# Query and memory-value projections in halves of 256 columns, two token blocks to a PSUM bank

## The chip, the cores and the metric

The kernel runs on one core of a Trainium2 chip. The metric is the device time of one execution in microseconds (us); smaller is better. TensorE (PE in the profile) multiplies and writes PSUM, VectorE (DVE), ScalarE (ACT) and GpSimd (POOL) work on tiles, and SyncE (SP) issues most of the DMAs. PSUM has eight banks, each 128 partitions by 512 fp32 columns.

## The reference

Two layers of a trunk over 256 latent and 256 context tokens, model width 1024. Each layer is a half-step SwiGLU block, three token mixers in parallel on one normalised input, and another SwiGLU block. The mixers are a windowed attention (A), a dense attention with RMS-normalised queries and keys (B) and a chunked mLSTM (C); one combined projection feeds all of them:

```python
def windowed_attention(q, k, v, k_ctx, v_ctx, sink): ...
def dense_attention(q, k_all, v_all):
    return blockwise_queries(lambda args: gqa_softmax(args[0], k_all, v_all, None, None), q)
IN_SIZES = (A_WIDTH, A_KV_WIDTH, A_KV_WIDTH, B_WIDTH, B_KV_WIDTH, B_KV_WIDTH, C_WIDTH, C_WIDTH, C_WIDTH, C_WIDTH, 4 * C_HEADS, N_BRANCH * D_MODEL)
```

The change concerns two pieces of 512 columns of that projection: the queries of branch B (`qb`, 8 heads of 64), which are squared and summed per head for the norm and rotated, and the values of the mLSTM (`vm`, 4 heads of 128). All arithmetic is fp32: each operand is split into a high and a low part, and a product is three matmuls.

## The kernel before, in words

**Tasks and units.** The work is a list of tasks. A task names the weight units that it needs, and `run_tasks` walks the list: SyncE loads units ahead into four raw buffers (512 KB each, L152), ScalarE rounds one to its high part (L162), VectorE takes the low part (L163), and the task's function emits its matmuls. `mm3` (L191) emits the three matmuls of a product, at L193 to L195.

**Order.** The code emits tasks one after another, and a scheduler then sets the order of each engine's instructions at compile time; a tile's readers and writers wait for each other by semaphores. PSUM tiles are whole banks of a pool of eight (`self.psum()`).

**The two projections.** `tok_tasks` makes four tasks for `qb` and four for `vm`. Task g takes two of the eight 128-row blocks of the model width, at all 512 columns. For each token block tb (four in layer 0; in layer 1 the context queries are not needed, so `qb` has two) it adds 2 x 3 matmuls of 512 columns into that block's own bank. After the fourth task `evac` empties each bank: for `qb` `q_rows` copies it on ScalarE (L760), squares it on ScalarE (L761), sums the squares of a head on VectorE (L762), and rotates latent blocks (L741, L746 twice, L747) or scales context blocks by the norm's gain (L772). For `vm` one copy, by turns on ScalarE (L200) and VectorE (L202).

**The attention woven around them.** `attn_steps` makes steps for each branch, token block and pair of heads. Step i holds score i, the transposes of step i-2 (`ATT_LAG`) and the product with V of step i-3. A score is two or three matmuls per head (L1016, mask L1018, L1019), the row maximum on VectorE (L1020, L1023), the exponential on ScalarE (L1034), the sink's term and the sum (L1039 to L1041), its reciprocal on VectorE (L1043) and the scaling of both heads on GpSimd (L1046). TensorE then transposes the scaled rows (L1058), ScalarE and VectorE split them (L188, L189), and TensorE multiplies by V (L1073, L1075). The queries of branch A come to score step 0 through `q_cols` (L779 transposes, L784 ScalarE, L785 VectorE). In layer 0 the remaining `qb` tasks and all `vm` tasks are woven between the first steps, with the mLSTM's gates (L1110 to L1190) and the merge gates (transposed products `fm`, evacuated at L1327); in layer 1 `qb` comes earlier and `vm` stands there.

Of the kernel before, what the change touches and what calls it, by code (L numbers as in the profile page):

```python
# [62 lines left out]
class Builder:  # L63
# [41 lines left out]
    def unit_src(self, key):  # L105
# [16 lines left out]
        if kind == "tok":  # L122
            _, l, name, ks, n = key
            src = a["w_" + name][l, ks[0] * P:(ks[-1] + 1) * P, :]
            return src.rearrange("(k p) c -> p k c", p=P), (len(ks), n), True
        if kind == "fm":
            _, l, j = key
            return a["w_fm"][l, j], (NK, P), True
# [566 lines left out]
    def tok_tasks(self, l, name, n, kper, tbs, ms, evac):  # L695
# [24 lines left out]
        return [mk(g) for g in range(ngroups)]  # L720

    def by_stream(self, tasks, pre):

        def fn(units):
            later = []
            for u, (_, t) in zip(units, tasks):
                t([u], [0, 1], later)
            pre(1)
            for evac, tb, ps in later:
                evac(tb, ps)  # L730
            for u, (_, t) in zip(units, tasks):
                t([u], [2, 3])
        return [([k for ks, _ in tasks for k in ks], fn)]
# [15 lines left out]
    def q_rows(self, q, src, tb, branch, ss):  # L749


        nc = self.nc
        if branch == 0:
            if tb < 2:
                self.rope(q, src, 8, tb, self.cos, self.sin)
            else:
                self.copy(q, src)
            return
        sq = self.t512()
        nc.scalar.activation(out=q, in_=src, func=AF.Copy)  # L760
        nc.scalar.activation(out=sq, in_=src, func=AF.Square)  # L761
        nc.vector.tensor_reduce(out=ss, in_=sq.rearrange("p (h d) -> p h d", d=64), axis=AX.X, op=ALU.add)  # L762
        if tb < 2:
            u = self.t512()
            self.rope(u, q, 8, tb, self.cosg[0], self.sing[0], q)
        else:
            self.times_g(q, q, 8, 0)

# [61 lines left out]
    def mixer_tasks(self, l, need_ctx, ms, pre, done, turn):  # L830
# [20 lines left out]

        def qq(x):
            def f(tb, ps):
                if f"qr{x}" not in R:
                    R[f"qr{x}"] = self.slot([P, 4, T])
                    if x:
                        R["qss"] = self.lp.tile([P, 4, 8], F32, tag="qss", name=self.nm("qss"))
                self.q_rows(R[f"qr{x}"][:, tb, :], ps, tb, x, R["qss"][:, tb, :] if x else None)
            return f

# [23 lines left out]

        def vm(tb, ps):
            if "vm" not in R:
                R["vm"] = self.slot([P, 4, 4, 129])
                nc.vector.memset(R["vm"][:, :, :, 128:129], 1.0)
            self.copy(R["vm"][:, tb, :, 0:128], ps.rearrange("p (h d) -> p h d", h=4))

# [10 lines left out]
        vt = self.tok_tasks(l, "vvg", 272, 2, range(4), ms, vv)  # L901
        qa = self.tok_tasks(l, "qa", 512, 2, qtb, ms, qq(0))
        qb = self.tok_tasks(l, "qb", 512, 2, qtb, ms, qq(1))
        conv = [self.conv_task(l, c, ms, R, need_ctx) for c in range(8)]

# [3 lines left out]
        kk_ = self.tok_tasks(l, "kk", 256, 4, range(4), ms, kk)  # L909
        vm_ = self.tok_tasks(l, "vm", 512, 2, range(4), ms, vm)  # L910
        if need_ctx:
# [538 lines left out]
def _layout(inp):  # L1450
# [20 lines left out]
    a["w_qa"] = c(w[:, :, C_QA + qcols])  # L1471
    a["w_qb"] = c(w[:, :, C_QB + qcols])
    a["w_kk"] = c(np.concatenate([w[:, :, C_KA:C_KA + 128], w[:, :, C_KB:C_KB + 128]], axis=2))
    gcols = np.concatenate([np.arange(0, 4), np.arange(8, 12), np.arange(4, 8), np.arange(12, 16)])
    a["w_vvg"] = c(np.concatenate([w[:, :, C_VA:C_VA + 128], w[:, :, C_VB:C_VB + 128], w[:, :, C_GM + gcols]], axis=2))
    a["w_vm"] = c(w[:, :, C_VM:C_VM + 512])
    a["w_om"] = c(w[:, :, C_OM:C_OM + 512])
# [42 lines left out]
```

## Time and profile before

| | |
|---|---|
| time, median of 3 runs | 2246.11 us (2245.70 to 2246.91) |
| the profiled execution's own time | 2245.83 us |
| its span in the profile | 2244.0 us |
| TensorE busy | 2186.8 us, 97% |
| VectorE busy | 1546.0 us, 69% |
| ScalarE busy | 997.9 us, 44% |
| GpSimd busy | 135.4 us, 6% |
| mean granted clock of TensorE | 0.992 |

The span is what the profiler covers; the profiled execution took 1.8 us more than it. Busy shares are means over all stages. The granted clock is 1.00 at TensorE's upper level, 2.4 GHz, and 0.50 at the lower, 1.2 GHz. Times in rows are microseconds from the start of the span, unless a duration is marked as ns. The changed tasks of layer 0 run from about 472 us, those of layer 1 (`vm`) from about 1760 us.

### The profile page before, as it was taken

Reading aid. Unit: us, or ns where it says so; the run is one execution under the profiler, and the core shown is the slowest. Engines: PE = TensorE matmul, PEld = TensorE weight load, DVE = VectorE, ACT = ScalarE, POOL = GpSimd, SP = SyncE. Lnnn points to the kernel's source line nnn. Section 1 sums busy time; section 2 is a strip of 40 time slices with the busy share of each in tenths; the row PEclk is TensorE's granted clock in tenths of the full one; section 3 lists DMA queues with packets and bytes.
Section 4 is the critical chain, followed back from the end, with each engine's and each line's share of the span. In section 5 each row is a group of like instructions: output and inputs, shape, how many; then the busy total and the mean of one; then the engine's idle time right before and its main releaser. Section 6 shows DMA issues by size and latency. Waiting matters only on the chain.

```text
span 2244.0 us, 30646 instructions
## 1 busy us (share of the span) xinstructions
PE 2186.8 (97%) x11666; PEld 1833.2 (82%) x11666; DVE 1546.0 (69%) x2760; ACT 997.9 (44%) x1594; POOL 135.4 (6%) x100
## 2 busy tenths in 40 slices
PE   7999999999999999999999999999999999998998
PEld 4877777787888888888878788777778888997997
DVE  4987775778576775664444378878858887876556
ACT  3322223545577833542222253222236468855444
POOL 0000000013152000000000000000000152000000
PEclk9999999999999999999999999999999999998999
DMA  7765564321213334434434236555744214565664
GB/s 285 226 197 182 165 200 146 123 94 68 92 51 113 122 120 143 142 112 133 139 104 134 101 118 197 189 187 181 222 138 152 85 67 126 183 217 173 193 190 155
DMA packets 127555, 334.52 MB, mean 149 GB/s; under 512 B 12840, under 2 KB 26216, under 8 KB 126640
## 3 DMA queue, kind: packets, MB, share of 16 engines
q1 hardware_dynamic: 112240, 315.60, 43.4%
q10 hardware_dynamic: 15168, 16.97, 2.4%
q8 instruction: 91, 1.49, 0.3%
q14 instruction: 56, 0.46, 0.1%
HBM read 322.48 MB, written 10.04 MB: 148 GB/s over the span
## 4 chain that ended last, share of the span: by engine, by line
PE 89%; DVE 6%; ACT 2%; issue 1%; DMA 1%; ACTq 0%; DVEq 0%
PE ps L193 27%; PE ps L194 27%; PE ps L195 27%; PE ps L1259 1%; PE ps L1058 1%; PE ps L1228 1%; PE ps L366 1%; DVE lo L163 1%; PE ps L1073 1%; PE ps L468 1%; PE ps L1075 1%; PE ps L1016 1%; DVE sm L1020 1%; DMA slot<-in_w_ada_dram 1%; PE ps L1019 1%
## 5 line engine op out<-in xcount | busy, mean ns | idle before, releaser
L162 ACT ACTIVATE hi<-raw 128x1024 fp32r<-128x1024 f32 (+1 forms) x444 | 457.4, 1032 | 770.7 <-PE ps L194 255.9
L193 PE MATMUL ps<-slot,hi 128*128 128x512 f32 (+1 forms) x2232 | 778.4, 351 | 6.0 <-ACT slot L188 4.9
L194 PE MATMUL ps<-slot,hi 128*128 128x512 f32 (+1 forms) x2232 | 775.6, 348 | 0.7 <-DVE slot L189 0.5
L195 PE MATMUL ps<-slot,lo 128*128 128x512 f32 (+1 forms) x2232 | 773.6, 347 | 0.0
L163 DVE TENSOR_TENSOR lo<-raw,hi 128x1024 fp32r<-128x1024 f32 (+1 forms) x444 | 526.7, 1190 | 232.3 <-ACT hi L162 230.6
L193 PEld LDWEIGHTS ps<-slot,hi 128*128 128x128 f32 x2232 | 420.5, 189 | 75.9 <-ACT slot L188 6.2
L195 PEld LDWEIGHTS ps<-slot,lo 128*128 128x128 f32 x2232 | 421.5, 189 | 57.4
L194 PEld LDWEIGHTS ps<-slot,hi 128*128 128x128 f32 x2232 | 421.5, 189 | 56.3 <-DVE slot L189 2.0
L193 PE MATMUL ps<-hi,slot 128*128 128x512 f32 (+2 forms) x1048 | 400.3, 382 | 1.9 <-ACT slot L188 1.1
L195 PE MATMUL ps<-hi,slot 128*128 128x512 f32 (+2 forms) x1048 | 398.8, 381 | 0.0
L194 PE MATMUL ps<-lo,slot 128*128 128x512 f32 (+2 forms) x1048 | 398.8, 381 | 0.0
L358 DVE SCALAR_TENSOR_TENSOR t<-raw,sc,t 128x1024 f32<-128x1024 f32 x224 | 280.3, 1281 | 129.9 <-DMA raw<-in_w_ada_dram 129.7
L1046 POOL TENSOR_SCALAR t<-t,sm 128x512 f32<-128x512 f32 (+1 forms) x96 | 135.2, 1420 | 1748.1 <-DVE sm L1043 1693.2
L193 PEld LDWEIGHTS ps<-hi,slot 128*128 128x128 f32 x1048 | 197.1, 188 | 46.2 <-issue 6.6
L195 PEld LDWEIGHTS ps<-hi,slot 128*128 128x128 f32 x1048 | 196.7, 188 | 39.8
L194 PEld LDWEIGHTS ps<-lo,slot 128*128 128x128 f32 x1048 | 197.0, 188 | 38.9 <-issue 0.2
L188 ACT ACTIVATE slot<-t 128x512 fp32r<-128x512 f32 (+1 forms) x138 | 80.5, 594 | 172.3 <-DVE t L606 153.5
L606 DVE TENSOR_TENSOR t<-ps,t 128x512 f32<-128x512 f32 (+1 forms) x88 | 54.7, 622 | 86.5 <-PE ps L195 85.2
L189 DVE TENSOR_TENSOR slot<-t,slot 128x512 fp32r<-128x512 f32 (+1 forms) x138 | 87.6, 643 | 5.1 <-ACT slot L188 4.6
L1020 DVE TENSOR_REDUCE sm<-ps 128x1 f32<-128x512 f32 (+1 forms) x96 | 54.1, 593 | 29.6 <-PE ps L1019 29.0
L603 ACT ACTIVATE t<-ps 128x512 f32<-128x512 f32 (+1 forms) x88 | 46.4, 527 | 24.2 <-DVE t L426 16.5
L189 DVE TENSOR_TENSOR t<-ps,t 128x512 fp32r<-128x512 f32 x80 | 54.2, 684 | 1.9 <-ACT t L188 1.7
(195 smaller groups left out, 1667.7 us busy)
## 6 DMA issues: line engine op xcount, KB each, us to landing
raw<-in_w_gu_dram SPq DMA_DIRECT2D x176, 512.0 KB
raw<-in_w_ada_dram SPq DMA_DIRECT2D x128, 512.0 KB
raw<-in_w_down_dram SPq DMA_DIRECT2D x92, 512.0 KB
raw<-in_w_fm_dram SPq DMA_DIRECT2D x64, 512.0 KB
raw<-in_w_br_dram SPq DMA_DIRECT2D x24, 512.0 KB
raw<-in_w_out_dram SPq DMA_DIRECT2D x24, 512.0 KB
slot<-in_w_ada_dram SPq DMA_DIRECT2D x16, 512.0 KB
raw<-in_w_down_dram SPq DMA_DIRECT2D x20, 256.0 KB
```

The lines of the kernel that those rows point to most:

```text
L162: self.nc.scalar.activation(out=hi, in_=raw, func=AF.Copy)
L163: self.nc.vector.tensor_tensor(out=lo, in0=raw, in1=hi.bitcast(F32), op=ALU.subtract)
L188: self.nc.scalar.activation(out=hi, in_=src, func=AF.Copy)
L189: self.nc.vector.tensor_tensor(out=lo, in0=src, in1=hi.bitcast(F32), op=ALU.subtract)
L193: mm(out, lh, rh, start=start, stop=False, **kw)
L194: mm(out, lh, rl, start=False, stop=False, **kw)
L195: mm(out, ll, rh, start=False, stop=stop, **kw)
L358: v.scalar_tensor_tensor(out=acc, in0=units[0], scalar=c, in1=acc, op0=ALU.mult, op1=ALU.add)
L603: nc.scalar.activation(out=hs["sg"][:, :W], in_=ps[:, :W], func=AF.Silu)
L606: nc.vector.tensor_tensor(out=hid[:, :W], in0=ps[:, :W], in1=hid[:, :W], op=ALU.mult)
L1020: v.tensor_reduce(out=mx[:, e:e + 1], in_=ps[:, :nkey], axis=AX.X, op=ALU.max)
L1046: nc.gpsimd.tensor_scalar(out=t[:, :nkey], in0=t[:, :nkey], scalar1=r[:, e:e + 1], scalar2=None, op0=ALU.mult)
```

## The change

`qb` and `vm` are made by a new `half_tasks`. There are still four units of 512 KB each, but a unit now holds four 128-row blocks at 256 columns: unit (h, g) is column half h, rows g. For each half the two units follow each other, and the half is evacuated after the second. Token blocks 0 and 1 share a bank (256 columns each), and so do 2 and 3; only the first matmul into a bank carries the start flag. The evacuation works on 256 columns, 4 query heads or 2 value heads at a time. The weights are laid out so that a unit is one contiguous piece per partition.

```diff
+        if kind == "half":
+            _, l, name, h, g = key
+            return a["w_" + name][l, h, g], (4, 256), True
...
+    def half_tasks(self, l, name, tbs, ms, evac):
+        ds = {}
+        def mk(h, g):
+            def fn(units):
+                u = units[0]
+                for tb in tbs:
+                    if g == 0 and tb % 2 == 0:
+                        ds[h, tb // 2] = self.psum().rearrange("p (b c) -> p b c", b=2)
+                    ps = ds[h, tb // 2][:, tb % 2, :]
+                    for x in range(4):
+                        lh, ll = ms["hi"][g][:, x, tb * P:(tb + 1) * P], ms["lo"][g][:, x, tb * P:(tb + 1) * P]
+                        self.mm3(ps, lh, ll, u[0][:, x, :], u[1][:, x, :], g == x == tb % 2 == 0, g == 1 and x == 3,
+                                 skip_group_check=True)
+                    if g:
+                        evac(tb, h, ps)
+            return ([("half", l, name, h, g)], fn)
+        return [mk(h, g) for h in range(2) for g in range(2)]
...
-        sq = self.t512()
+        sq = self.t512()[:, :256]
...
-            self.rope(u, q, 8, tb, self.cosg[0], self.sing[0], q)
+            self.rope(u, q, 4, tb, self.cosg[0], self.sing[0], q)
...
-            self.times_g(q, q, 8, 0)
+            self.times_g(q, q, 4, 0)
...
-            self.copy(R["vm"][:, tb, :, 0:128], ps.rearrange("p (h d) -> p h d", h=4))
+            self.copy(R["vm"][:, tb, 2 * h:2 * h + 2, 0:128], ps.rearrange("p (h d) -> p h d", h=2))
...
-        qb = self.tok_tasks(l, "qb", 512, 2, qtb, ms, qq(1))
+        qb = self.half_tasks(l, "qb", qtb, ms, qqb)
...
-        vm_ = self.tok_tasks(l, "vm", 512, 2, range(4), ms, vm)
+        vm_ = self.half_tasks(l, "vm", range(4), ms, vm)
...
+    halves = lambda m: c(m.reshape(2, 2, 4, P, 2, 256).transpose(0, 4, 1, 3, 2, 5))
-    a["w_qb"] = c(w[:, :, C_QB + qcols])
+    a["w_qb"] = halves(w[:, :, C_QB + qcols])
-    a["w_vm"] = c(w[:, :, C_VM:C_VM + 512])
+    a["w_vm"] = halves(w[:, :, C_VM:C_VM + 512])
```

The scheduler then orders the engines differently. Line numbers of the changed kernel are 3 higher at `mm3` (L196 to L198), 25 higher in `q_rows` and `q_cols`, and 27 higher in the attention. The number of instructions on SyncE is the same; TensorE has 336 more matmuls in all, VectorE 26 more instructions, ScalarE 16 more.

*TensorE, layer 0, in front of the first transposes.* Before, from the first `qb` matmul on there are 72 matmuls of 512 columns and the three score steps 0 to 2, and these rows end that stretch; `ps_3834` is token block 3's bank of `qb`, `t_628` and `t_629` are the two heads' rows of step 0, which GpSimd has scaled:

```order
L195 MATMUL ps_3834<-hi_3920,slot_3117 128x512
L193 MATMUL ps_3834<-hi_3920,slot_3115 128x512
L194 MATMUL ps_3834<-lo_3921,slot_3115 128x512
L195 MATMUL ps_3834<-hi_3920,slot_3117 128x512
L1058 MATMUL ps_3976<-ident,t_628_3855 128x128 [waits PE_49,Activation_49,Pool_49]
L1058 MATMUL ps_3976<-ident,t_629_3857 128x128 [waits Pool_49]
L1058 MATMUL ps_3976<-ident,t_628_3855 128x128
L1058 MATMUL ps_3976<-ident,t_629_3857 128x128
L193 MATMUL ps_3813<-hi_4178,slot_3115 128x512
```

Now there are 72 matmuls of 256 columns and the same score steps. `ps_3838` is the bank of blocks 2 and 3, `ps_4029` and `ps_4034` are score step 2, and `t_626` and `t_627` are step 0's rows:

```order
L198 MATMUL ps_3838<-hi_3697,slot_3117 128x256
L1043 MATMUL ps_4029<-slot_3741,slot_3770 128x512 [waits DVE_49,PE_49]
L1045 MATMUL ps_4029<-maskr,identr 128x256
L1046 MATMUL ps_4029<-slot_3741,slot_3770 128x512
L1043 MATMUL ps_4034<-slot_3741,slot_3770 128x512 [waits DVE_49,PE_49]
L1045 MATMUL ps_4034<-maskr,identr 128x256
L1046 MATMUL ps_4034<-slot_3741,slot_3770 128x512
L1085 MATMUL ps_4054<-ident,t_626_3877 128x128 [waits PE_49,Pool_49]
```

The 16 `qb` matmuls that stood between score step 2 and the transposes have moved behind them; the transposes now follow score step 2 directly. Their waits (Pool, Activation) are the same.

*TensorE, layer 0, directly behind those transposes.* `ps_4075` is a merge gate of 512 columns and `ps_3813` the bank of token blocks 0 and 1, here block 1's second unit; before, no `qb` matmul of a first use waits in this way:

```order
L1085 MATMUL ps_4061<-ident,t_627_3879 128x128
L196 MATMUL ps_4075<-slot_3114,hi_3807 128x512 [waits PE_49,Activation_49]
L197 MATMUL ps_4075<-slot_3116,hi_3807 128x512
L198 MATMUL ps_4075<-slot_3114,lo_3808 128x512
L196 MATMUL ps_3813<-hi_3697,slot_3115 128x256 [waits Activation_49]
```

The new wait on Activation is for ScalarE's reading of block 0's half in the same bank.

*VectorE, layer 0, around score step 0.* Before, all eight pieces of `q_cols` stand ahead of the row maxima (L1020) of step 0, and `lo` is the low part of a weight unit:

```order
L785 TENSOR_TENSOR slot_3770<-ps_3798,slot_3770 64x4x128 [waits Activation_49]
L1020 TENSOR_REDUCE sm_3843<-ps_3844 128x1 [waits PE_49]
L1020 TENSOR_REDUCE sm_3843<-ps_3849 128x1 [waits PE_49]
L1110 TENSOR_TENSOR s_632_3867<-gm_3709,gateb_3237 128x64
L1023 SCALAR_TENSOR_TENSOR sm_3841<-sm_3843,nsink_3233 128x2 [waits DVE_49]
L163 TENSOR_TENSOR lo_3991<-raw_3701,hi_3990 128x1024 [waits DMAHW1_49]
L1039 TENSOR_TENSOR sm_3859<-sinkr_3235,sm_3841 128x2 [waits DVE_49]
L1113 SCALAR_TENSOR_TENSOR s_633_3869<-s_632_3867 128x32
L1128 COPY s_637_3890<-s_632_3867 128x4x4 x2
```

Now one piece of `q_cols` (L810) stands between the two maxima (L1047), and the gain's multiplication of one `qb` half (L797, `slot_3960`) ahead of the sink's term (L1066) and of what follows:

```order
L1047 TENSOR_REDUCE sm_3865<-ps_3866 128x1 [waits PE_49]
L810 TENSOR_TENSOR slot_3770<-ps_3798,slot_3770 64x4x128 [waits Activation_49]
L1047 TENSOR_REDUCE sm_3865<-ps_3871 128x1 [waits PE_49]
L1137 TENSOR_TENSOR s_630_3889<-gm_3709,gateb_3237 128x64
L1050 SCALAR_TENSOR_TENSOR sm_3863<-sm_3865,nsink_3233 128x2 [waits DVE_49]
L797 TENSOR_TENSOR slot_3960<-slot_3960,gqk_3231 128x256 [waits Activation_49]
L1140 SCALAR_TENSOR_TENSOR s_631_3891<-s_630_3889 128x32 [waits DVE_49]
L1155 COPY s_635_3912<-s_630_3889 128x4x4 x2
L1066 TENSOR_TENSOR sm_3881<-sinkr_3235,sm_3863 128x2 [waits DVE_49]
L166 TENSOR_TENSOR lo_4069<-raw_3701,hi_4068 128x1024 [waits DMAHW1_49]
L166 TENSOR_TENSOR lo_4172<-raw_3811,hi_4171 128x1024 [waits DMAHW2_49]
```

The rest of the first half's evacuation (L787, L766, L771, L772 in the new numbers) stands in the rows up to score step 3; before, all of `qb`'s evacuation stood behind score step 6.

## Rows read from the trace of the kernel before

**Rows 1.** The page: busy time of each engine, and the last chain's shares.

```profile
PE 2186.8 (97%) x11666; PEld 1833.2 (82%) x11666; DVE 1546.0 (69%) x2760; ACT 997.9 (44%) x1594; POOL 135.4 (6%) x100
...
PE 89%; DVE 6%; ACT 2%; issue 1%; DMA 1%; ACTq 0%; DVEq 0%
```

**Rows 2.** TensorE's waits, 480 to 620: us in total, times, longest.

```profile
PE ps L1058 <- DVE t L189: 2.5, 2, 2.0
PE ps L1073 <- ACT t L1034: 2.2, 1, 2.2
```

**Rows 3.** Windows of layer 0: stretch, length, busy PE, PEld, DVE, ACT, POOL, clock, DMA.

```profile
472.60:494.50 21.90, 21.14 (x94) 16.25 (x93) 20.61 (x48) 11.62 (x23) 3.92 (x2) 1.00 0.18 55
494.50:524.30 29.80, 29.80 (x171) 24.12 (x169) 22.68 (x62) 15.12 (x34) 12.51 (x8) 1.00 0.12 46
524.30:526.50 2.20, 0.02 (x2) 0.01 (x1) 2.03 (x5) 0.84 (x3) 0.00 (x0) 1.00 0.14 54
...
527.10:530.50 3.40, 3.40 (x15) 2.92 (x14) 1.95 (x5) 2.02 (x5) 2.65 (x2) 0.50 0.73 274
```

**Rows 4.** Timeline, 472 to 495: start, us, instruction [idle before it <- releaser].

```profile
472.62 0.48 PE L193 MATMUL ps<-hi,slot 128*128 128x512 f32 x1
...
481.71 0.19 PEld L1016 LDWEIGHTS ps<-slot,slot 128*128 128x128 f32 x1 [0.41 <-DVE slot L785]
...
490.37 3.92 POOL L1046 TENSOR_SCALAR t<-t,sm 128x512 f32<-128x512 f32 x2 [489.94 <-DVE sm L1043]
...
494.47 0.60 PE L1058 MATMUL ps<-ident,t 128*128 128x128 f32 x4
```

**Rows 5.** Timeline of TensorE, two busy stretches, first and last row of each.

```profile
453.73 0.28 PE L194 MATMUL ps<-lo,slot 128*128 128x256 f32 x1
...
460.30 0.28 PE L193 MATMUL ps<-hi,slot 128*128 128x256 f32 x1
...
2099.78 0.39 PE L195 MATMUL ps<-hi,slot 128*128 128x512 f32 x1
...
2105.79 0.39 PE L194 MATMUL ps<-lo,slot 128*128 128x512 f32 x1
```

**Rows 6.** Groups by line and shape: x count, busy us, mean ns, idle before.

```profile
L193 PEld LDWEIGHTS ps<-hi,slot 128*128 128x128 f32 x1048 | 197.1, 188 | 46.2 <-issue 6.6 <-ACT slot L188 1.3 <-ACT t L478 0.2
...
L606 DVE TENSOR_TENSOR t<-ps,t 128x512 f32<-128x512 f32 x66 | 45.4, 688 | 72.1 <-PE ps L195 71.4 <-ACT t L603 0.7
...
L606 DVE TENSOR_TENSOR t<-ps,t 128x256 f32<-128x256 f32 x22 | 9.3, 425 | 14.4 <-PE ps L195 13.9 <-ACT t L603 0.5
```

**Rows 7.** Timeline of layer 1, 1780 to 1827.

```profile
1780.04 3.10 POOL L1046 TENSOR_SCALAR t<-t,sm 128x512 f32<-128x512 f32 x2 [1074.99 <-DVE sm L1043]
...
1787.80 1.03 PE L1058 MATMUL ps<-ident,t 128*128 128x128 f32 x8
...
1826.48 0.37 PE L1190 MATMUL ps<-ident,ZN 128*32 128x128 f32 x1 [0.42 <-DVE ZN L1185]
```

**Rows 8.** Windows of layer 1, columns as in rows 3.

```profile
1766.50:1787.80 21.30, 20.34 (x105) 15.19 (x104) 20.13 (x51) 10.40 (x22) 6.05 (x4) 1.00 0.15 53
1787.80:1816.40 28.60, 26.41 (x191) 24.12 (x190) 26.28 (x63) 17.25 (x39) 13.18 (x9) 1.00 0.24 82
1816.40:1826.50 10.10, 7.74 (x59) 6.60 (x58) 8.55 (x21) 7.77 (x20) 5.34 (x4) 0.88 0.00 0
1826.50:1831.00 4.50, 4.50 (x22) 4.50 (x23) 0.28 (x1) 0.09 (x1) 2.56 (x2) 0.50 0.37 124
```

**Rows 9.** The last chain in layer 0: start, us, engine and what it writes.

```profile
523.23 1.14 DVE sm L1020 x2
...
536.59 0.69 DVE qss L762
...
542.20 0.60 DVE qss L762
...
544.65 0.66 PE ps L1058 x4
```

More of the change, by code (lines that the diff above doesn't have):

```diff
@@ L763, in q_rows @@
         if tb < 2:
-            u = self.t512()
-            self.rope(u, q, 8, tb, self.cosg[0], self.sing[0], q)
+            u = self.t512()[:, :256]
+            self.rope(u, q, 4, tb, self.cosg[0], self.sing[0], q)
         else:
-            self.times_g(q, q, 8, 0)
+            self.times_g(q, q, 4, 0)
     def times_g(self, dst, src, nh, w):
@@ L850, in vv, with qqa, qqb @@
             self.copy(R["gm"][:, tb, :], ps[:, 256:272])
[L852 to L859, printed above, removed]
+        def qqa(tb, ps):
+            if "qr0" not in R:
+                R["qr0"] = self.slot([P, 4, T])
+            self.q_rows(R["qr0"][:, tb, :], ps, tb, 0, None)
+        def qqb(tb, h, ps):
+            if "qr1" not in R:
+                R["qr1"] = self.slot([P, 4, T])
+                R["qss"] = self.lp.tile([P, 4, 8], F32, tag="qss", name=self.nm("qss"))
+            self.q_rows(R["qr1"][:, tb, 256 * h:256 * h + 256], ps, tb, 1, R["qss"][:, tb, 4 * h:4 * h + 4])
         def qcols(x):
@@ L883, in unspill, with vm @@
                 nc.sync.dma_start(self.X[s], self.spill[s])
-        def vm(tb, ps):
+        def vm(tb, h, ps):
             if "vm" not in R:
@@ L901, in mixer_tasks @@
         vt = self.tok_tasks(l, "vvg", 272, 2, range(4), ms, vv)
-        qa = self.tok_tasks(l, "qa", 512, 2, qtb, ms, qq(0))
-        qb = self.tok_tasks(l, "qb", 512, 2, qtb, ms, qq(1))
+        qa = self.tok_tasks(l, "qa", 512, 2, qtb, ms, qqa)
+        qb = self.half_tasks(l, "qb", qtb, ms, qqb)
         conv = [self.conv_task(l, c, ms, R, need_ctx) for c in range(8)]
```

## The prediction

> **What bounds the kernel now.** Read the page first: TensorE is busy 97% of the span, VectorE 69%, and 89% of the chain that ended last is TensorE's [rows 1]. So the time is TensorE's work plus the little that it idles or runs at half clock. A change that leaves the number of multiplied columns alone, as this one does, can move the time in three ways only: through the spacing of its matmuls, through TensorE's idle time, and through its clock.
>
> Next the waits of TensorE around the changed code in layer 0. Behind the first transposes it waits 2.5 us for VectorE's L189 and 2.2 us for ScalarE's exponential L1034 [rows 2]. The windows show where: the 21.90 us from the first query matmul to the first transposes and the 29.8 us after them are all but full (21.14 and 29.80 us busy), then comes a hole of 2.2 us (0.02 us busy), and 3.4 us at a granted clock of 0.50 behind it [rows 3]. The engine had been idle before the clock fell. Those 4.7 us of idling and 3.4 / 2 = 1.7 us at the lower of the two levels (1.2 instead of 2.4 GHz) are all that TensorE loses here: 6.4 us.
>
> The timeline of the first attention step shows that it only just fits. The query projection starts at 472.62, score step 0 follows at 481.71 after a wait of 0.41 us for VectorE's L785, and GpSimd's two scalings of that step run from 490.37 for 3.92 us, to 494.29. The first transposes, which read the scaled rows, start at 494.47 [rows 4]. TensorE arrives there with its own work 0.2 us after GpSimd is done: a cover with nothing to spare.
>
> **The change, part by part.** *Spacing.* 336 matmuls of 512 columns (48 + 96 for qb, 96 + 96 for vm) become 672 of 256. In a busy stretch 27 rows of 512 columns start from 2099.78 to 2105.79, 26 steps of 0.2312 us; 57 rows of 256 columns from 453.73 to 460.30, 56 steps of 0.1173 us [rows 5]. Two halves cost 0.0034 us more than a whole: 336 x 0.0034 = 1.1 us, 0.65 of it in layer 0 (192 wholes), 0.5 in layer 1 (144).
>
> A weight load takes 188 ns in its own rows [rows 6], longer than the 117 ns that a half matmul lasts, and the change doubles the loads; yet in the 256-column stretch, with a load for each matmul, the pace held: 56 loads of 188 ns would be 10.5 us one after another and lie in 6.57, so they overlap. The Trainium skill speaks against the change here: "TensorE: Matmul & The Clock Gate", section "Back-to-back issue gap", says that in a stream of load and matmul pairs the gap is set by both operations, and gives about 81 ns at 128 columns and 131 ns at 512. Interpolated (an estimate from that page), two halves would cost some 60 ns more than one whole, and the sum would gain 20 us instead of 1.1. The trace's two gaps differ by a factor of 1.97 and disagree; I take the trace.
>
> *Evacuation.* Each query block is copied, squared, reduced and rotated in two pieces, each memory value block copied in two. VectorE pays 688 ns for 512 columns and 425 for 256 [rows 6], so a split costs 2 x 0.425 - 0.688 = 0.16 us for each instruction more. There are 26 more in the order: 16 in layer 0 (4 reductions, 8 for the rotation of two blocks, 2 scalings, 2 of the 4 copies), 2.6 us, and 10 in layer 1, 1.6 us. ScalarE pays about 1 us per layer. ScalarE has room. For VectorE the windows decide: it is busy 20.61 of 21.9 us before the first transposes [rows 3], so what lands there delays the step.
>
> *Bank sharing.* With two blocks in a bank, block 1's second unit is ordered behind ScalarE's read of block 0 (the wait on Activation in the order). The rows of before show no such wait. Below, it costs nothing, since other matmuls can run meanwhile in the order. Above, four ScalarE reads of 256 columns, about 0.4 us each, would stand bare per bank pair: 2 us. In the order three 512-column matmuls stand between the transposes and the waiting one, and TensorE is there late anyway; I take nothing, and keep 2 us for the range.
>
> *Order, the main term.* Before, 72 wholes and three score steps stand between the start of qb and the first transposes; now 72 halves and the same score steps. TensorE reaches the transposes 72 x (0.2312 - 0.1173) = 8.2 us earlier by its own work. But the scalings on GpSimd that it must wait for do not come earlier: they hang on score step 0, and that on VectorE's L785, for which TensorE waits already [rows 4]. In VectorE's order one 256-column multiplication by the gain now stands in front of the step's L1041: +0.4 us (0.425, the 256-column row). So TensorE idles 8.2 + 0.4 = 8.6 us before the transposes, part of it perhaps already before score step 0.
>
> The 8.2 us of matmuls are not lost; they are queued behind the transposes. They can fill what TensorE wastes there now: 4.7 us idle and 1.7 us at half clock, 6.4 us. They cannot be repaid a second time, so 2.2 us stay. A hole of 8 us is also several times the 2.2 us after which the clock fell in the trace, so I count one new stretch like that one: 3.4 us at 0.50, +1.7 us. One more would be +1.7 again; none, 0.
>
> Layer 0: 8.6 + 0.65 - 6.4 + 1.7 = +4.55 us.
>
> *Layer 1.* Before, 76 vm wholes stand ahead of the first transposes (17.6 us), now 96 halves (11.3): 6.3 us less. GpSimd's scaling ends at 1783.14 and the transposes run at 1787.80 [rows 7], so 4.66 us of that are harmless; the bare hole is at least 1.6 us, at most 6.3 (VectorE is busy 20.13 of 21.3 us there [rows 8], and half copies now stand in it). What comes back: TensorE idles 2.19 us in the window after the transposes and 2.36 in the next, and then runs 4.5 us at 0.50 (2.25 us lost) [rows 8]. Those holes end at VectorE's chain to L1185, released at 1826.48 [rows 7]. If the deferred matmuls fill them so that the clock stays up, the end gains 2.25 us; VectorE's 1.6 us of extra work go the other way. I take both: -0.65.
>
> **Sum.** 4.55 + 0.5 (spacing, layer 1) - 0.65 = +4.4 us. On the profiled execution's 2245.83 that is 2250.2; the three runs' median of 2246.11 is 0.3 us above it, so 2250 to 2250.5, and I say 2250.
>
> **The rivals.** *B: the hole is not repaid.* The stalls behind the transposes are VectorE's: the chain there runs L1020 at 523.23, the reductions of qb from 536.59 to 542.20, and reaches TensorE at 544.65 [rows 9]. If VectorE's chain sets the end of the phase, TensorE having fallen behind, deferred matmuls do not fit into the old holes. Then 8.6 + 0.65 + 1.7 remain in layer 0, +11: 2257. For it speaks VectorE's share (22.68 of 29.8 us); against, that half of the query's evacuation now lies before that chain, not in it.
>
> *C, the other side: everything is repaid.* The rows show 4.7 + 1.7 us in layer 0 and 0.96 + 2.19 + 2.36 + 2.25 us in layer 1 for deferred matmuls to fill, 14.2 us, and with the 0.76 idle in layer 0 before the transposes 14.9. The least holes are 8.6 and 1.6 us, the spacing 1.1: 11.3 - 14.9 = -3.6 us, 2242; with GpSimd at layer 1's pace (3.10 instead of 3.92 us) 2241.5. It needs layer 1's chain to L1185 to come no later than now; from a shift of 2 us of that chain on it is a rival no more. For it speaks that the banks of two blocks instead of four are held, so later steps find free banks sooner.
>
> *D: nothing but the spacing.* If TensorE's order counts for less than I think, because the scalings come earlier by as much as the matmuls do, 1.1 us remain: 2247. Against it: VectorE stands at 20.61 of 21.9 us [rows 3], so score step 0 has nowhere to go.
>
> *E: the loads set the pace*, at 188 ns each, one after another: 336 x (2 x 0.188 - 0.2312) = +49 us, 2295 at the most; the nearest row at the other end is the pace held at 0.1173, and nothing lies between. The 256-column rows speak against it, so it has 0.02. The Trainium skill's page named above would put this rival at about 2266.
>
> **How the numbers follow.** A (the sum) 0.48, own range 2246.5 to 2254: no second cold stretch or two, bare waits of 2 us. B 0.20, C 0.18, D 0.12, E 0.02. The range 2240 to 2258 holds A, C, D and most of B. A measurement tells 0.2%, 4.5 us, from no change: 2241.6 to 2250.6. Faster: two thirds of C, 0.12. Same: the rest of C, D, half of A, 0.43. Slower: the other half of A, B and E, 0.45.
>
> **What would show it.** Right: an idle stretch of 6 to 9 us on TensorE in front of the first transposes of layer 0, released by GpSimd's L1046 (its new line) or split with score step 0; a stretch at 0.50 behind it; the waits on L189 and L1034 smaller than 2.5 and 2.2 us; 256-column gaps of 0.117 us in the new matmuls. Wrong, if the hole is under 3 us, if GpSimd's scalings come several us earlier after the first query matmul than the 17.75 us of now (490.37 - 472.62), if the waits behind the transposes keep their size, or if gaps of the new matmuls are above 0.13 us.

## The result and the profile after

The changed kernel takes 2260.56 us (median of 4 runs, 2259.23 to 2261.86) against 2246.51 us before (4 runs, 2245.70 to 2248.20): a ratio of 1.0055, 95% interval 1.0043 to 1.0067, so 9.7 to 15.1 us slower. The forecast was 2250, with 2258 as its upper end. The profiled execution has a span of 2258.0 us (before 2244.0) and a mean granted clock of 0.990.

The page after, which answers to [rows 1]:

```profile
PE 2194.5 (97%) x12002; PEld 1856.9 (82%) x12002; DVE 1548.1 (69%) x2788; ACT 999.9 (44%) x1610; POOL 136.6 (6%) x100
...
PE 87%; DVE 6%; ACT 3%; DMA 2%; issue 1%; ACTq 0%; DVEq 0%
```

TensorE is still the bound; its share of the last chain fell by two points. Of its waits from 480 to 640 us (columns as in [rows 2]) the two of [rows 2] are gone; 0.7 us for the exponential (now L1061) remain, which stood in the trace of before as well, at another matmul than in [rows 2]. The largest is now for GpSimd's scaling:

```profile
PE ps L1085 <- POOL t L1073: 6.3, 2, 5.5
PE ps L196 <- DVE slot L810: 1.7, 1, 1.7
PE ps L1043 <- DVE slot L810: 1.5, 1, 1.5
PE ps L196 <- ACT t L1061: 0.7, 1, 0.7
```

The timeline of the first attention step of layer 0 after, against [rows 4]: first query matmul, score step 0, scaling, transposes. The last row is a later wait, new as well.

```profile
473.79 0.36 PE L196 MATMUL ps<-hi,slot 128*128 128x256 f32 x1
...
481.08 0.47 PE L1043 MATMUL ps<-slot,slot 128*128 128x512 f32 x1 [1.48 <-DVE slot L810]
...
491.96 3.11 POOL L1073 TENSOR_SCALAR t<-t,sm 128x512 f32<-128x512 f32 x2 [491.53 <-DVE sm L1070]
...
493.57 0.69 PE L1085 MATMUL ps<-ident,t 128*128 128x128 f32 x2 [5.46 <-POOL t L1073]
...
592.64 0.36 PE L196 MATMUL ps<-hi,slot 128*128 128x256 f32 x1 [1.75 <-DVE slot L810]
```

The hole stands where it was forecast, in two parts: 1.48 us before score step 0 and 5.46 us before the transposes, with 0.86 us more inside them (the second wait on L1073). That is 7.8 us. The windows of the changed kernel (columns as in [rows 3]; first layer 0, then layer 1) show the clock:

```profile
473.80:493.60 19.80, 12.86 (x94) 11.52 (x91) 18.91 (x43) 10.67 (x22) 1.64 (x2) 0.91 0.16 48
493.60:523.40 29.80, 28.94 (x187) 25.73 (x188) 24.61 (x71) 13.44 (x32) 11.10 (x7) 0.89 0.12 40
489.60:499.80 10.20, 5.37 (x21) 4.68 (x22) 7.97 (x33) 4.91 (x15) 6.38 (x4) 0.52 0.18 53
1774.00:1796.00 22.00, 17.59 (x126) 15.62 (x125) 20.50 (x54) 10.82 (x24) 6.01 (x4) 0.92 0.16 52
...
1820.00:1838.00 18.00, 15.72 (x122) 14.47 (x120) 14.62 (x34) 12.58 (x29) 6.71 (x4) 0.91 0.19 60
1838.00:1842.00 4.00, 3.85 (x20) 3.85 (x21) 0.61 (x4) 0.23 (x1) 3.10 (x2) 0.54 0.02 4
```

The clock is at half from 490.0 to 500.3 us (the window shown begins 0.4 us earlier), after TensorE had begun to idle, for three times the length of the stretch in [rows 3]; but TensorE is busy for only 5.8 us of it. In layer 1, where [rows 7] showed no idle time ahead of the transposes, the longest wait is now at score step 0, and two stretches at half clock lie in the phase: 3.4 us right behind that wait, and 6.8 us from 1834.9 us on. TensorE's waits from 1700 to 1860 us, the three largest:

```profile
PE ps L1043 <- DVE slot L810: 4.4, 1, 4.4
PE ps L1102 <- DVE t L192: 1.6, 1, 1.6
PE ps L196 <- ACT slot L191: 0.5, 1, 0.5
```

The timeline of the longest, with VectorE's piece of the queries that it waits for:

```profile
1782.13 0.68 DVE L810 TENSOR_TENSOR slot<-ps,slot 64x512 fp32r<-64x512 f32 x1
...
1782.96 0.47 PE L1043 MATMUL ps<-slot,slot 128*128 128x512 f32 x1 [4.41 <-DVE slot L810]
...
1794.69 1.03 PE L1085 MATMUL ps<-ident,t 128*128 128x128 f32 x8
```

The same place before, where score step 0 already waited a little; L785 is the later L810:

```profile
1765.74 1.04 PE L779 MATMUL ps<-ident,slot 128*128 128x128 f32 x8
...
1770.08 0.69 DVE L785 TENSOR_TENSOR slot<-ps,slot 64x512 fp32r<-64x512 f32 x1
...
1772.08 0.47 PE L1016 MATMUL ps<-slot,slot 128*128 128x512 f32 x1 [0.70 <-DVE slot L826]
```

**Where the 14 us are.** I cut both traces at the same instructions and divided each stretch into three: time in which no TensorE row runs (idle), half of the busy time at a clock of 0.50 (lost to the clock), and the rest. "Layer 0" is the stretch from the transposes at 434.0 us to those of an attention step at 642.9 us (times of before), "layer 1" the one from 1708.3 to 1860.1 us; of the last SwiGLU block it is 2063.6 to 2230.6 us. Microseconds; "diff" is the stretch's length less that of before, each from one execution.

```
               layer 0                    layer 1                    last block
               diff  idle   clock rest    diff  idle   clock rest    diff
before           -    7.79  1.71 199.43     -    7.20  3.00 141.63     -
change         +5.1  11.55  2.91 199.56   +3.1   7.93  4.65 142.40   +3.3
change again   +4.2  11.55  1.82 199.69   +2.9   7.99  4.28 142.44   +3.3
qb_only        +2.7  10.20  1.89 199.49   +0.3   6.43  2.93 142.77   +0.2
vm_only        +1.7   9.29  1.71 199.67   +7.9  11.29  7.34 141.13   +2.9
pair_evac      +2.3   9.78  3.03 198.39   +6.1  10.79  5.64 141.48   +3.3
own_banks      +3.2   9.56  2.88 199.71   +5.8  11.56  4.21 141.90   +3.3
rows_only      +3.8   9.91  2.80 200.02   +5.3  11.51  3.25 142.37   +1.1
rows_pair      -3.0   6.00  0.00 199.95   +2.4   7.92  5.12 141.15   +1.1
qb_rows_pair   -2.7   6.24  0.00 200.01   +0.2   7.07  2.91 142.09   +0.3
split_evac     +1.9   7.89  3.37 199.55   +0.3   7.09  3.25 141.81    0.0
fill_hole      +3.3   9.56  3.91 198.78   +2.4   7.96  4.08 142.23   +3.3
fill_between   +3.2   9.00  3.17 199.91   +2.4   7.94  4.35 141.96   +2.9
before_slots   +0.8   7.15  3.41 199.20   +2.2   7.64  4.81 141.56   +2.5
```

The three places give 11.5 us, and 10.4 in the second execution, which is inside the interval of 9.7 to 15.1 us. Of the 14.0 us between the two spans about 1 us more lies in the SwiGLU block ahead of the last mixers (the last section comes back to it). 1.2 us lie before 434 us, where no mixer has run yet and the other profiles are 1.6 us later on average than the one of before: that execution merely started well. The clock column varies by some 2 us with where the stretches at half clock fall (before_slots, whose mixers are those of before, has 3.41 and 4.81 us); between the change's two executions idle and rest agree to 0.2 us. The profiled execution of `rows_pair` (2248.01 us) was the slowest of its 11.

### The profile page after: what moved, and what is told of

It reads as the page before. It is cut to its first block, busy times and chain, and to the rows that moved or that the text cites. A ratio compares the mean times of both kernels' runs of the same rounds, so it can differ in the third digit from the quotient of the medians.

```text
span 2258.0 us, 31371 instructions
## 1 busy us (share of the span) xinstructions
PE 2194.5 (97%) x12002; PEld 1856.9 (82%) x12002; DVE 1548.1 (69%) x2788; ACT 999.9 (44%) x1610; POOL 136.6 (6%) x100
## 4 chain that ended last, share of the span: by engine, by line
PE 87%; DVE 6%; ACT 3%; DMA 2%; issue 1%; ACTq 0%; DVEq 0%
PE ps L196 27%; PE ps L197 27%; PE ps L198 26%; PE ps L1286 1%; DVE lo L166 1%; PE ps L1085 1%; ACT hi L165 1%; PE ps L369 1%; PE ps L1255 1%; PE ps L1102 1%; PE ps L1100 1%; DVE sm L1047 1%; PE ps L471 1%; PE ps L1043 1%; PE ps L1046 1%
## 5 line engine op out<-in xcount | busy, mean ns | idle before, releaser
L196 PE MATMUL ps<-slot,hi 128*128 128x512 f32 (+1 forms) x2232 | 779.3, 351 | 6.2 <-ACT slot L191 5.1
L198 PE MATMUL ps<-slot,lo 128*128 128x512 f32 (+1 forms) x2232 | 774.7, 348 | 0.0
L196 PEld LDWEIGHTS ps<-slot,hi 128*128 128x128 f32 x2232 | 420.3, 189 | 74.6 <-ACT slot L191 6.4
L198 PEld LDWEIGHTS ps<-slot,lo 128*128 128x128 f32 x2232 | 421.6, 189 | 58.0
L196 PE MATMUL ps<-hi,slot 128*128 128x512 f32 (+2 forms) x1160 | 421.0, 363 | 3.7 <-DVE slot L810 1.7
L197 PE MATMUL ps<-lo,slot 128*128 128x512 f32 (+2 forms) x1160 | 417.8, 360 | 0.0
L198 PE MATMUL ps<-hi,slot 128*128 128x512 f32 (+2 forms) x1160 | 417.5, 361 | 0.0
L196 PEld LDWEIGHTS ps<-hi,slot 128*128 128x128 f32 x1160 | 218.7, 189 | 46.7 <-issue 7.2
L198 PEld LDWEIGHTS ps<-hi,slot 128*128 128x128 f32 x1160 | 218.4, 188 | 36.1 <-DVE slot L192 0.2
L197 PEld LDWEIGHTS ps<-lo,slot 128*128 128x128 f32 x1160 | 218.9, 189 | 35.1
L1073 POOL TENSOR_SCALAR t<-t,sm 128x512 f32<-128x512 f32 (+1 forms) x96 | 136.4, 1432 | 1758.1 <-DVE sm L1070 1682.0
L1047 DVE TENSOR_REDUCE sm<-ps 128x1 f32<-128x512 f32 (+1 forms) x96 | 54.2, 593 | 26.3 <-PE ps L1046 25.7
```

Source lines behind the costliest of these rows:

```text
L196: mm(out, lh, rh, start=start, stop=False, **kw)
L197: mm(out, lh, rl, start=False, stop=False, **kw)
L198: mm(out, ll, rh, start=False, stop=stop, **kw)
L1047: v.tensor_reduce(out=mx[:, e:e + 1], in_=ps[:, :nkey], axis=AX.X, op=ALU.max)
L1073: nc.gpsimd.tensor_scalar(out=t[:, :nkey], in0=t[:, :nkey], scalar1=r[:, e:e + 1], scalar2=None, op0=ALU.mult)
```

## The experiments

Two explanations stood against each other at first: the order of TensorE's work around score step 0, which opens the hole, and the work itself (halves, their weight loads, VectorE's pieces). Later runs take up what the first had shown.

**One projection alone.** `qb_only` leaves `vm` whole, `vm_only` leaves `qb` whole.

```diff
-        vm_ = self.half_tasks(l, "vm", range(4), ms, vm)
+        vm_ = self.tok_tasks(l, "vm", 512, 2, range(4), ms, vm)
```

> Only qb in halves; vm whole, as before. Theory H (the loss is the holes that TensorE has in front of the first attention steps because less work stands there): the hole of 6 us in layer 0 with its half-clock stretch is there (+5 us), the hole of 4.4 us at score step 0 of layer 1 is gone: 2251 to 2253. Rival W (the halves cost by themselves, by their matmuls and their extra evacuations, 14 us over 336 wholes): 144 of 336 wholes are halved, +6, 2252.5, and spread over the halves, not in a hole. Rival R (the last SwiGLU block of layer 2 loses 3.3 us by slower 256-column matmuls, 0.1185 instead of 0.1153 us, and this belongs to the program's layout, not to the change): the step there says which of the two it is, 3.3 us either way.

> Only vm in halves; qb whole. H: layer 0 keeps its order up to the first transposes, no hole there; the 4.4 us hole at score step 0 of layer 1 stays: +3, 2249 to 2250. W: 192 of 336 wholes are halved, +8, 2254.5. R: the step of the 256-column matmuls in the last block is 0.115 or 0.118, 3.3 us either way.

Measured: `qb_only` 2250.24 us against 2248.39, ratio 1.0008 (0.9999 to 1.0017); `vm_only` 2259.85, 1.0053 (1.0040 to 1.0066). The forecast's main term sits with `qb`, and there it is: the same waits of 6.3 and 1.5 us, +2.7 us in layer 0. `vm_only`, expected at 2249 to 2250 us, was a miss: it is as slow as the change. But it does not lose in the same places. In layer 0 the two losses add up to the change's (2.7 + 1.7 against 4.2 to 5.1 us); in layer 1 `vm_only` loses 7.9 us where the change loses 3. Its waits from 1700 to 1860 us begin with two, of which the change has only the second, at 4.4 us; before, the step of L1043 waited 0.7 us:

```profile
PE ps L1167 <- DVE s L1156: 4.1, 1, 4.1
PE ps L1043 <- DVE slot L810: 3.1, 1, 3.1
```

**The shared bank.** `pair_evac` reads a bank only when both of its blocks are complete; `own_banks` gives each block and half a bank of its own.

```diff
-                    if g:
-                        evac(tb, h, ps)
+                    if g and tb % 2:
+                        for e in (tb - 1, tb):
+                            evac(e, h, ds[h, e // 2][:, e % 2, :])
```

```diff
-                    if g == 0 and tb % 2 == 0:
-                        ds[h, tb // 2] = self.psum().rearrange("p (b c) -> p b c", b=2)
-                    ps = ds[h, tb // 2][:, tb % 2, :]
+                    if g == 0:
+                        ds[h, tb] = self.psum()
+                    ps = ds[h, tb][:, :256]
...
-                        self.mm3(ps, lh, ll, u[0][:, x, :], u[1][:, x, :], g == x == tb % 2 == 0, g == 1 and x == 3,
+                        self.mm3(ps, lh, ll, u[0][:, x, :], u[1][:, x, :], g == x == 0, g == 1 and x == 3,
```

> As the change, but a bank is read only when both of its blocks are complete, so no matmul waits for a read in its bank; 96 instead of 72 halves stand before the first transposes of layer 0. H: the hole there shrinks by 24 x 0.117 = 2.8 us, from 6.3 to about 3.5 us behind GpSimd and with it one half-clock stretch: 2256 to 2258. W: no change, 2260.

> The change with a bank for each block and half, so no matmul waits for a read of its neighbour; order of units as in the change, 96 halves ahead of the first transposes of layer 0 as in pair_evac. H: as pair_evac, layer 0's loss 2 to 3 us instead of 4 to 5, 2258 to 2262 in all, since layer 1's hole stays. Rival S (the reads in a shared bank are what costs in the change): 2250 or less.

Measured: 2261.39 us against 2248.39, 1.0056 (1.0042 to 1.0069), and 2261.78 us against 2247.46, 1.0063 (1.0050 to 1.0076). Neither is better than the change, so `pair_evac` was a miss. In layer 0 both gain 1 to 3 us on it: without the wait for the read of block 0, 48 halves instead of 24 stand between score step 0 and the transposes in `pair_evac`, and the wait there is 3.9 instead of 6.3 us. In layer 1 both lose as much, through the first of the waits of `vm_only`; in `own_banks` it is

```profile
PE ps L1167 <- DVE s L1156: 5.2, 1, 5.2
```

So sharing the bank is not, in this order, what costs the 14 us.

**The order of the units.** The change runs both units of half 0, then both of half 1. `rows_pair` runs the rows first, both halves of a unit pair before the next rows, with the evacuation of `pair_evac`; `rows_only` has the same order and evacuates block by block, as the change does; `qb_rows_pair` is `rows_pair` with `vm` whole.

```diff
-        return [mk(h, g) for h in range(2) for g in range(2)]
+        return [mk(h, g) for g in range(2) for h in range(2)]
```

> As the change, with halves and shared banks, but the units go by rows first (rows 0 of both halves, then rows 1), so both halves of a projection are evacuated at its end, after their pair; 136 halves (16.0 us) stand before the first transposes of layer 0, before there were 72 wholes (16.7 us). H: no hole over 2 us in layer 0 and a smaller one in layer 1: 2247 to 2251. W: the same 672 halves and the same split evacuations: 2258 to 2260.

> As the change, but units go rows first; each block is still evacuated as soon as it is complete, so the reads of a shared bank still stand before the second block's matmuls. 130 halves (15.2 us) stand before the first transposes of layer 0, against 136 in rows_pair and 72 in the change. H, if what counts is the number of matmuls there: within 2 us of rows_pair, 2245 to 2248. Rival S (the waits for the reads in a shared bank are what costs): the waits are as in the change, so more than half of the 14 us remains, 2254 and more.

> vm whole as before; qb in halves and shared banks, rows first and evacuated after the pair. H (holes by the order): no hole in layer 0 as in rows_pair (4.4 us better there than qb_only's +2.7), layer 1 as in before, without rows_pair's +2.4: 3 to 5 us below before, 2243 to 2245. W (the halves themselves cost): 144 halved wholes, +6. R: a step of 0.115 or 0.118 us in the last block moves it by up to 3.3 us and is read separately.

Measured: `rows_pair` 2245.05 us against 2248.39, 0.9988 (0.9979 to 0.9996); `rows_only` 2257.47 against 2248.17, 1.0040 (1.0026 to 1.0053); `qb_rows_pair` 2245.36 against 2248.17, 0.9985 (0.9977 to 0.9994). `rows_pair` makes the same matmuls of 256 columns as the change, with the same loads and the same pieces on VectorE, and is 15.5 us below its median: the work is not the cause. In the two profiles 8.1 us of the difference lie in layer 0; 2.2 us lie in the last block and 1 us in the one ahead of the last mixers, where `rows_pair` has before's buffers (last section), so these are not the order's. About 88 halves (10.3 us) now stand between score step 0 and the transposes. `qb_rows_pair`, with the same cover in layer 0, waits from 470 to 660 us for

```profile
PE ps L1044 <- DVE slot L811: 1.5, 1, 1.5
PE ps L1086 <- DVE t L192: 1.0, 2, 0.6
PE ps L1044 <- ACT t L1062: 0.8, 1, 0.8
PE ps L196 <- ACT t L1062: 0.7, 1, 0.7
PE ps L1086 <- POOL t L1074: 0.5, 1, 0.5
```

(its lines are one higher). The wait for GpSimd is 0.5 us, no stretch at half clock is left in layer 0, and the layer is 2.7 us shorter than before. `rows_only` was a miss. Order alone does not do it. 82 halves stand between score step 0 and the transposes, and the wait for GpSimd is down to 0.3 us, but TensorE's waits from 470 to 660 us become many small ones:

```profile
PE ps L1100 <- DVE t L192: 1.7, 1, 1.7
PE ps L1043 <- ACT t L1061: 1.7, 1, 1.7
PE ps L1043 <- DVE slot L810: 1.5, 1, 1.5
PE ps L1085 <- DVE t L192: 1.3, 1, 1.3
```

The evacuation once for a pair is all that the two differ in, and it is worth 12.4 us between their medians. So reading the blocks of a shared bank one by one does cost in this order, as the rival in the expectation had it, in which four banks fill at the same time. By which path is not shown: the second block's matmuls stand behind the read of the first, but VectorE's pieces also fall at other times, and a rows-first order with a bank for each block was not run.

**VectorE's pieces by themselves.** `split_evac` keeps the whole matmuls of before and evacuates each bank in two pieces.

```diff
+        two = lambda f: lambda tb, ps: [f(tb, h, ps[:, 256 * h:256 * h + 256]) for h in range(2)]
+        qb = self.tok_tasks(l, "qb", 512, 2, qtb, ms, two(qqb))
...
+        vm_ = self.tok_tasks(l, "vm", 512, 2, range(4), ms, two(vm))
```

> Before's whole matmuls, task order and one bank per block; only the evacuations are split in two pieces of 256 columns. H: the order in front of the first transposes of both layers is that of before, so no hole: 0 to +3 us, the 26 extra instructions of VectorE at 0.16 us (4.2 us in all) being hidden in part. W, in the form that the split evacuation is what costs: most of the 14 us, +10 and more.

Measured: 2249.35 us against 2248.17, 1.0005 (0.9996 to 1.0014). By this interval VectorE's and ScalarE's additional instructions cost between -1 and +3 us.

**The change once more.** A second profile, for its scatter.

> The change once more, for a second profile. If the slower 256-column step in the last block (0.1185 us; before 0.1153) belongs to the program, it is 0.118 again; if it belongs to the execution, it can be 0.115 and the span 3 us shorter. The holes in both layers and their sizes must come back: about 6 us in layer 0 behind GpSimd, about 4 us at score step 0 of layer 1.

Measured: 2258.99 us, a span of 2257.1. Idle time is the same to 0.06 us in both layers; the stretches at half clock moved by 1 us. The new waits are therefore of the program, not of the execution.

**Filling the hole.** `fill_hole` moves a merge-gate task (24 matmuls of 512 columns, 5.5 us by [rows 5]) ahead of score step 0 in the list; `fill_between` moves it behind score step 1.

```diff
-            side, with_conv, with_mem = weave(side, pre_[0]), pre_[1][:PRE], pre_[1][PRE:]
+            side, with_conv, with_mem = weave(side, pre_[0][1:]), pre_[1][:PRE], pre_[1][PRE:]
...
+        if need_ctx:
+            out += pre_[0][:1]
```

```diff
-        out += weave(att[:na], side) + weave(att[na:], weave(conv, with_conv))
+        k0 = 2 if need_ctx else 0
+        out += att[:k0] + (pre_[0][:1] if need_ctx else []) + weave(att[k0:na], side) + weave(att[na:], weave(conv, with_conv))
```

> The change with nothing altered but the place of one merge-gate task of layer 0: its 24 matmuls of 512 columns (5.5 us) stand ahead of score step 0 instead of behind the first transposes. H: layer 0's hole of 5.5 + 0.9 us behind GpSimd and the 1.5 us at score step 0 shrink by about 5 us and one half-clock stretch goes; layer 1 stays (4.4 us hole): 2255 to 2257 against the change's 2260. W (halves cost by themselves) or a bound by VectorE's chain: no change, 2259 to 2261.

> The change, with the merge-gate task of fill_hole moved again: its 24 matmuls of 512 columns now stand between score step 1 and the first transposes of layer 0, so 17 halves and 24 wholes (2.0 + 5.5 = 7.5 us) lie between score step 0 and the transposes; in the change 24 halves (2.8 us), in before 39 wholes (9.0 us), in fill_hole 24 halves. Refined theory H2 (the hole is the time from score step 0 to GpSimd's end minus TensorE's work between score 0 and the transposes): the hole behind GpSimd falls from 6.3 to about 1.5 us, and layer 0 loses 0 to 1.5 us instead of 4 to 5: 2255 to 2257. First theory H (what counts is the work from the start of qb): fill_hole had the same sum of work and kept 4.1 us of hole, so this keeps it too, 2259.

Measured: 2259.51 us against 2247.46, 1.0049 (1.0035 to 1.0062), and 2256.34 against 2247.85, 1.0036 (1.0022 to 1.0049). `fill_hole` missed. Its timeline (two lines higher):

```profile
486.08 0.40 PE L1045 MATMUL ps<-slot,slot 128*128 128x512 f32 x1
...
495.68 0.69 PE L1087 MATMUL ps<-ident,t 128*128 128x128 f32 x2 [3.13 <-POOL t L1075]
...
497.32 1.54 PE L1087 MATMUL ps<-ident,t 128*128 128x128 f32 x6 [0.95 <-POOL t L1075]
```

The work went in front of score step 0, moved the step to 486.08 us, and with it VectorE's and GpSimd's part; 4.1 us of the hole stayed. `fill_between` puts it where it covers, between score step 0 and the transposes:

```profile
481.93 0.47 PE L1044 MATMUL ps<-slot,slot 128*128 128x512 f32 x1 [1.48 <-DVE slot L810]
...
494.43 0.33 PE L1086 MATMUL ps<-ident,t 128*128 128x128 f32 x1 [0.75 <-POOL t L1074]
...
496.72 0.98 PE L1086 MATMUL ps<-ident,t 128*128 128x128 f32 x7 [1.72 <-POOL t L1074]
...
503.03 0.98 PE L1086 MATMUL ps<-ident,t 128*128 128x128 f32 x7 [1.21 <-POOL t L1074]
```

The wait is down from 6.3 to 2.5 us, but the next step waits for GpSimd too, 1.6 us in all, and layer 0 is only 1 to 2 us shorter than with the change. Behind this one hole stands the next.

**The same program in other buffers.** All variants with the slow last block have moving operands there in other buffers than before. `before_slots` is the kernel before, with one unused buffer taken from the pool ahead of that block, so that the operands move.

```diff
             st["hi"] = [self.slot([P, 4, T], F32R) for _ in range(2)]
+            if l == 1 and k == 2:
+                d = self.slot([P, 4, T])
+                nc.gpsimd.memset(d[:, 0, 0:1], 0.0)
             st["lo"] = [self.slot([P, 4, T], F32R) for _ in range(2)]
```

> The kernel before with one unused buffer taken from the pool of long-lived tiles in front of the last SwiGLU block; the instructions stay, but the normed tokens of that block lie in other buffers than 12, 8 (and 2, 0). Theory R2 (the pace of 256-column matmuls depends on the buffers that hold the two parts of the moving tokens): the step in the last block leaves 0.1153 us and becomes 0.117 to 0.119, +2 to +3.5 us, 2250. Rival (the pace hangs on something else of the changed programs): 0.1153 again and no change in time.

Measured: 2250.56 us against 2247.46, 1.0013 (1.0004 to 1.0021): 3.1 us slower by the placement of operands alone, 2.5 us of it read in the last block.

## Why the prediction was wrong

**What bounds.** "In three ways only: through the spacing of its matmuls, through TensorE's idle time, and through its clock" holds. The step that failed was to count the spacing of the changed matmuls alone. The last SwiGLU block is not touched by the diff, and each of its matmuls on the first pair of operand buffers starts 0.0060 us later after the one before (0.1197 instead of 0.1137 us in 505 steps): 3.0 of its 3.3 us. The change makes tiles live at other times, so the pool hands out other buffers there. `before_slots` shows that this is enough. No rival of mine held it, and with these 3.3 us the sum would have been 7.7 instead of 4.4.

**Spacing and loads.** 0.65 + 0.5 us were forecast; the rest column says +0.1 to +0.3 in layer 0 and +0.8 in layer 1. Rival E, the loads as the pace, is refuted: 192 loads more leave the rest of layer 0 at 199.6 us, and the changed matmuls start 0.117 us after one another, as forecast. The same holds for the estimate of 20 us from the Trainium skill, "TensorE: Matmul & The Clock Gate", section "Back-to-back issue gap": no run here shows it.

**Evacuation.** VectorE has 28 instructions more on the page (2788 against 2760), not the 26 counted ahead of the run; the two more are in layer 1, 0.3 us by the same working. That the split would delay the step by one multiplication, 0.4 us, was too little. From score step 0 to the start of the scaling it was 490.37 - 481.71 = 8.66 us [rows 4] and is 491.96 - 481.08 = 10.88 us: 2.2 us more. GpSimd's 3.11 instead of 3.92 us gave 0.8 back, and score step 0 stands 7.29 instead of 9.09 us behind the first query matmul, which I had excluded when I put rival D down. The errors cancel, and the hole is 7.8 us for a forecast of 8.6: that it came so close is luck.

**Bank sharing.** I took nothing and kept 2 us. The cost is not in bare waits for ScalarE's reads. What the order fixes instead is how many halves may stand between score step 0 and the transposes: the second unit's odd blocks wait for the read of their bank, and half 1 comes only after half 0 is evacuated. So 24 halves (2.8 us) stand there instead of 39 wholes (9.0 us).

**Order in layer 0.** Forecast +4.55, measured +5.1 and +4.2. Idle time rose by 3.76 us; the forecast's own was 8.6 - 4.7 = 3.9, and the old waits behind the transposes did go. The new stretch at half clock came with the hole. The mechanism was right, and `qb_rows_pair` shows it from the other side: with cover for the step, layer 0 is 2.7 us shorter than before. The size is partly luck: `qb_only` has the whole hole and loses 2.7 us, and the rest came with `vm`, which no term of layer 0 held beyond its spacing (the wait of 1.75 us at 592.64 us is one of `vm_only` too). Of rival B, the hole not repaid, `fill_between` bears out a part: with most of the hole filled TensorE waits for GpSimd again at the next step. Its price of 11 us did not come.

**Layer 1.** Forecast -0.15 with its spacing (0.5 - 0.65), measured +2.9 to +3.1. This is the second step that failed, by its size and by its sign. I argued that 4.66 us of the earlier arrival are harmless because GpSimd's scaling is early there, and looked at the transposes. The wait came a step sooner, at score step 0: TensorE is there after 24 halves (2.8 us) behind the transposes of `q_cols` instead of 20 wholes (4.6 us), VectorE's L810 is not done, and it idles 4.41 instead of 0.70 us. That is half of it. The other half is VectorE's order, which I did not read there: before, a piece L785 came after two of the four pieces of the keys (L826); now all four (L851) stand ahead of the first L810, and score step 0 starts 8.3 us behind the first of those transposes instead of 6.3. Most of the hole is repaid (idle +0.7, and +0.8 in the rest, of which 0.5 was forecast as spacing). The half-clock stretch at the end of the phase, which I let vanish (-2.25), stayed at 6.83 us, and one of 3.41 us came right behind the hole in both executions. The clock's share of the +3, 1.3 to 1.65 us, is nevertheless no more than scatter: `before_slots`, with the mixers of before, has 10.24 us at half clock there too.

**The rivals.** C, everything repaid, fell with the layer 1 term. The code changes that would have made it true are `rows_pair` and `qb_rows_pair`, at 0.9988 and 0.9985. D, nothing but the spacing, is refuted by the 3.76 us of idle time. The sum by what was measured: 4.2 to 5.1 + 2.9 to 3.1 + 3.3 = 10.4 to 11.5 us, where 4.4 stood, and 1 us more with the block ahead of the last mixers.

**What stays open.** Why VectorE's L1156 comes 4 to 6 us late in layer 1 of `vm_only`, `pair_evac` and `own_banks`, and not in the change, was not pursued. Nor is it shown how much of layer 1's 3 us is the hole and how much the scatter of the clock. And nothing here says why one placement of operands is quicker than another.

## What to carry to other kernels

When a step of one engine hangs on a chain through the others, count the work that may legally stand between its two ends: smaller pieces and shared banks decide that, and the same matmuls in another order, with each bank read once, moved this kernel from 1.0055 to 0.9988 of its old time. Look for the wait at every link of the chain, not only at the last one. In a kernel that TensorE fills to 97%, compare the pace of code that the change does not touch as well: there lay 4 of the 14 us.

## What the runs showed that I had not expected

The pace of a busy stream of 256-column matmuls depends on which buffers hold its moving operands. The windows below are 20 us from the last block, of four kernels: before, the change, before with the unused buffer, and `qb_rows_pair`. TensorE is busy throughout at a clock of 1.00 in all of them, with the DMA at about the same rate; only the number of matmuls differs.

```profile
2060.00:2080.00 20.00, 20.00 (x176) 20.00 (x175) 12.42 (x15) 9.75 (x16) 0.00 (x0) 1.00 0.64 205
```

```profile
2070.00:2090.00 20.00, 20.00 (x171) 20.00 (x171) 11.89 (x16) 10.27 (x16) 0.00 (x0) 1.00 0.61 199
```

```profile
2065.00:2085.00 20.00, 20.00 (x172) 20.00 (x171) 11.99 (x15) 9.42 (x14) 0.00 (x0) 1.00 0.58 198
```

```profile
2058.00:2078.00 20.00, 20.00 (x176) 20.00 (x175) 12.42 (x15) 9.88 (x16) 0.00 (x0) 1.00 0.64 205
```

Taken over the whole block, from neighbouring rows of the trace (a few records are missing) and the buffers' numbers in the built program (a pool of 13 buffers, 8256 bytes apart in each partition; the high and the low part of the normed tokens, first four of the eight 128-row blocks of the model width):

```
                                     high, low buffer   us per step (505 steps)
before                               12, 8              0.1137
qb_rows_pair                         12, 8              0.1139
rows_pair                            12, 8              0.1151
vm_only                              12, 9              0.1182
fill_between                         12, 1              0.1182
before_slots                          8, 2              0.1178
change, twice                        12, 7              0.1197, 0.1196
```

The other four blocks (518 steps) run at 0.1170 to 0.1179 in all of them, so the quick pair is the exception and not the rule: before had it by luck, and any change that shifts the pool's turns can lose it. The pair is not all of it: `rows_pair` has before's and is 0.0014 us slower.

The block ahead of the last mixers shows the same, less strongly, at 512 columns. Its three streams of 264, 336 and 336 such matmuls take 219.8 us, from the first start to the last of each, in before and in the five other kernels with the same four buffers there (`before_slots` is one of them). In the change, twice, they take 220.8 us, with one of the buffers 7 instead of 8, and in the six other variants, all with other buffers, 220.6 to 221.5 us. That is the 1 us left over above. It does not follow from the buffers' numbers alone: in the block behind the first mixers the change has 7 instead of 8 as well, and the same three streams take 219.4 us for 219.6 before. No run moved these buffers by themselves.
